# Planes of the split weight tiles 64 bytes longer: another SBUF alignment for each buffer

## The chip, the cores and the metric

The kernel runs on one core of a Trainium2 chip. The metric is device time in microseconds of one execution. Five engines work in parallel and wait for one another by semaphores: PE (TensorE, the matmuls), DVE (VectorE), ACT (ScalarE), POOL (GpSimd) and SP, which here issues most of the DMAs. SBUF is the on-chip memory with 128 partitions; an address below is the byte offset of a tile within each partition. PSUM receives the matmuls' results.

## The reference

One layer of a diffusion backbone in float32: 512 latent tokens of width 1024, 256 context tokens, 8 query and 2 key/value heads of 128.

```
hx = modulate(rms_norm(x, norm1_g), sh1, sc1)        # sh, sc, g from silu(c) @ w_mod
qx, kx, vx, ux, gx = project(hx, w_in)               # 1024 -> 4608; q, k normed, rotary
attn = block_attention(qx, [kc, kx], [vc, vx])       # softmax over 768 keys
y_a = attn @ w_attn_out
y_b = silu(layer_norm(depthwise_conv(glu(ux), 31))) @ w_conv_out
x = x + g1 * ((sigmoid(g_a) * y_a + sigmoid(g_b) * y_b) @ w_out)
hx2 = modulate(rms_norm(x, norm2_g), sh2, sc2)
x = x + g2 * ((gelu(depthwise_conv(a, 3)) * b) @ w_down)   # a, b = hx2 @ w_up, 2 x 2816
return rms_norm(x, final_g)
```

## The kernel before

Every large product is made of three matmuls in the type float32r. A float32 operand is split into a high part (a cast to float32r by ACT, line 181) and a low part (source minus high part, by DVE, line 182), and `mm3` (lines 202 to 206) adds high x high, high x low and low x high into one PSUM bank. So each step over 128 input channels is three matmuls, on lines 204, 205 and 206, mostly with 512 moving columns, and before each of them its own stationary operand of 128 x 128 is loaded (PEld in the rows).

The weights arrive in chunks of 8 KB per partition in `raw` tiles (three buffers). `weights` (line 192) splits a chunk into tiles named hl: two planes of 1024 floats, the high part and the low part, in four buffers that are taken in turn. An hl tile is stationary where the output has channels on the partitions (gates, attention output, up projection: out<-s,hl in the rows, the moving operand first) and moving where the output has tokens on the partitions (queries, output projection, down projection: out<-hl,s). The other operand is nearly always one of the 19 slots s0 to s18 (two planes of 512 floats), which hold the activations. A few others play that part in places: ex, e0 and e1 (ex holds one of four channel blocks of the convolution and later one block of the output projection, and all three are among the 14 places for the activations of the feed-forward part), and in the attention stage va (values), pT (high parts of the transposed probabilities) with y or plo (their low parts; y also holds the low parts of the values).

The stages follow each other in the program's order, with the convolution's taps on DVE laid under the projections and the attention: modulation and projections, attention (about 125 to 290 us of the span), gates and branches (to about 430), output projection and norm, up and down projection in three groups of 11, 7 and 4 channel blocks. The order on each engine is fixed when the program is built.

Where a tile lies follows from the order in which the pools are opened. At the bottom of SBUF a scratch area for DMA descriptors is reserved (16,384 bytes by default), then 128 bytes of constants; then come the four hl buffers, the slots, the cb tiles, vectors and small tiles, and the rest. The starts before:

| tile | start | length | start modulo 512 |
|---|---|---|---|
| hl, four buffers | 16512, 24704, 32896, 41088 | 8192 | 128, 128, 128, 128 (both planes) |
| s0 to s18 | 49280, then every 4096 | 4096 | 128 |
| cb0 to cb3 | 127104, then every 4224 | 4224 | 128, 256, 384, 0 |
| ident, ones | 145216, 145728 | 512 | 320 |
| va | 147680, ... | 512 | 224 |
| raw, y, plo, ex, e0, e1, pT, tmp | from 158560 on | | 352 |

All offsets of a matmul's operands within these tiles are multiples of 512 bytes, so that the start of an operand modulo 512 is that of its plane.

Of the kernel before, what the change touches and what calls it, by code (L numbers as in the profile page):

```python
# [10 lines left out]
F32R = mybir.dt.float32r  # L11
# [4 lines left out]
P = 128  # L16
# [143 lines left out]
def body(tc, x_d, ctx_d, wts_d, vecs_d, rows_d, rope_d, out_d, at):  # L160
    nc = tc.nc
# [3 lines left out]
    def pool(name, bufs=1, stack=es, **kw):  # L165
        return stack.enter_context(tc.tile_pool(name=name, bufs=bufs, reuse_waits="tile", **kw))
# [4 lines left out]
    hlp = pool("hlp")  # L171
# [8 lines left out]
    def split(src, hi, lo):  # L180
        a = S.copy(hi, src)  # L181
        b = V.tensor_tensor(lo, src, hi.bitcast(F32), ALU.subtract)  # L182
        return a.ins, b.ins

    def fetch(name, n=CH):
        raw = wp.tile([P, CH], F32, tag="raw", name="raw", bufs=3)
        nc.sync.dma_start(raw[:, :n], wts_d[at[name], :, :n])
        return raw
# [3 lines left out]
    def weights(name, w, n=CH):  # L192
        raw = fetch(name, n)
        out = []
        for o in range(0, n, 1024):
            m = min(1024, n - o)
            t = hlp.tile([P, 2, 1024], F32R, tag="hl", name="hl", bufs=4)
            done[:] = split(raw[:, o : o + m], t[:, 0, :m], t[:, 1, :m])
            out.append(t[:, :, :m].rearrange("p a (k c) -> p a k c", c=w))
        return out  # L200
# [169 lines left out]
    with ExitStack() as p0:  # L370
# [101 lines left out]
        for op in FIRST.split():  # L472
            n = int(op[1])
            if op[0] == "x":
                for t in range(TT):
                    nc.sync.dma_start(xt[t], x_d[tok(t), :])
                for t in range(TT):
                    normed(xt[t], xt[t], flat(slot[8 + t]))
            elif op[0] == "m":
                mod_x(n)  # L480
            elif op[0] == "r":
                with ExitStack() as q:
                    for i in after:
                        q.enter_context(tc.issue_after(i))
                    rows_x(n)
            elif op[0] == "w":
                wu[n] = weights(("u", n), P)
                after = list(done)
            else:
                u_mm("ab".index(op[0]), (2 * n, 2 * n + 1))  # L490
# [70 lines left out]
        for k in range(4):  # L561
            split(raw[:, 512 * k : 512 * k + 512], qT[k][:, 0], qT[k][:, 1])
        wk = qT[0:4], weights(("kv", 1), 512)
        for t in range(TT):
            project(pk[t], wk[0], hx, 0, t)
# [21 lines left out]
        def conv_u(i):  # L587
            w = weights(("u", i), P)
            for g in range(2):
                o = acc()  # L590
                for k in range(KT):
                    mm3(o, w[g][:, :, k], hx[k], k == 0, k == KT - 1)
                    if k == 3:
                        yield
                if g == 0:
                    tb = glu_b(o)
                else:
                    glu_a(i, tb, o)
                yield
# [21 lines left out]
        t = 0  # L621
# [16 lines left out]
    with ExitStack() as p1:  # L638
# [49 lines left out]
        t = 0  # L688
# [372 lines left out]
```

## Time and profile before

| | us |
|---|---|
| median of 3 runs | 840.84 (840.52 to 840.9) |
| profiled execution | 838.52 |
| its span, first to last instruction | 836.7 |
| PE busy | 818.0 |
| DVE busy | 566.5 |
| ACT busy | 362.1 |
| mean granted clock of PE | 0.998 |

The span is what the trace covers. Busy time is the time in which an engine has at least one instruction under way; matmuls overlap one another, so a busy PE says little on what one matmul costs. For that one reads the starts: the distance in time from the start of a matmul to that of the next is called a step below. PEld, the loading of stationary operands, runs beside the matmuls.

### The profile page before, as it was taken

The page shows a single profiled execution, that of the slowest core. Times are in us where ns is not written, and L with a number is a line of the kernel's source. Part 1 is how long each engine was busy: PE and PEld are TensorE (multiplying, and loading weights), DVE is VectorE, ACT ScalarE, POOL GpSimd, SP SyncE. Part 2 cuts the span into 40 slices and gives each one's busy share as a digit, 9 for nine tenths or more (in the row PEclk, how much of TensorE's full clock was granted, in tenths as well). Part 3 has the DMA queues.
Part 4 walks back from the last instruction along what each step waited for, and adds up shares of the span by engine and source line. Part 5 has one row for each costly group of instructions (what it writes and reads, how often), then busy time and mean ns, then how long its engine had stood idle before and what let it go on. Part 6 is the DMA issues. An engine that isn't in the chain of part 4 may idle for free.

```text
span 836.7 us, 10190 instructions
## 1 busy us (share of the span) xinstructions
PE 818.0 (98%) x3948; PEld 669.3 (80%) x3948; DVE 566.5 (68%) x979; ACT 362.1 (43%) x700; POOL 25.2 (3%) x50
## 2 busy tenths in 40 slices
PE   6999999999999999999999999999999999999995
PEld 2588888878888888888878988888888888888884
DVE  2578878999999997963855377755244555346565
ACT  3454455789776223523515653333122333213333
POOL 1001010000000000000000000000000000000001
PEclk9999999999999999999999999999999999999999
DMA  8861112020102336573730124542222222222102
GB/s 358 307 268 49 51 56 96 4 99 1 51 1 105 126 149 250 209 280 115 259 144 0 52 101 151 201 151 88 89 101 101 100 101 89 89 100 101 51 1 101
DMA packets 16177, 99.25 MB, mean 119 GB/s; under 512 B 1792, under 2 KB 2048, under 8 KB 6144
## 3 DMA queue, kind: packets, MB, share of 16 engines
q1 hardware_dynamic: 15120, 95.98, 31.1%
q10 hardware_dynamic: 1008, 2.62, 0.9%
q8 instruction: 31, 0.51, 0.2%
q14 instruction: 18, 0.15, 0.1%
HBM read 96.49 MB, written 2.10 MB: 118 GB/s over the span
## 4 chain that ended last, share of the span: by engine, by line
PE 91%; DVE 4%; ACT 2%; DMA 1%; issue 1%; POOL 0%; POOLq 0%; SPq 0%
PE acc L204 24%; PE acc L206 24%; PE acc L205 24%; PE bank L205 3%; PE bank L206 3%; PE bank L204 3%; PE tr L715 2%; DMA raw<-in_wts 1%; PE sc L204 1%; PE sc L206 1%; PE sc L205 1%; PE acc L426 1%; DVE s L182 1%; PE acc L431 1%; PE tr L403 1%
## 5 line engine op out<-in xcount | busy, mean ns | idle before, releaser
L204 PE MATMUL acc<-s,hl 128*128 128x512 f32 (+1 forms) x632 | 242.0, 384 | 0.6 <-ACT s L181 0.6
L206 PE MATMUL acc<-s,hl 128*128 128x512 f32 (+1 forms) x632 | 239.5, 379 | 0.0
L205 PE MATMUL acc<-s,hl 128*128 128x512 f32 (+1 forms) x632 | 239.3, 379 | 0.0
L182 DVE TENSOR_TENSOR hl<-raw,hl 128x1024 fp32r<-128x1024 f32 x118 | 139.1, 1185 | 77.4 <-ACT hl L181 76.9
L181 ACT CAST hl<-raw 128x1024 fp32r<-128x1024 f32 x118 | 119.4, 1021 | 148.9 <-PE acc L206 126.9
L204 PEld LDWEIGHTS acc<-s,hl 128*128 128x128 f32 x632 | 118.7, 188 | 23.6 <-issue 1.0
L205 PEld LDWEIGHTS acc<-s,hl 128*128 128x128 f32 x632 | 119.1, 188 | 22.7 <-issue 1.2
L206 PEld LDWEIGHTS acc<-s,hl 128*128 128x128 f32 x632 | 119.0, 188 | 22.5
L532 DVE SCALAR_TENSOR_TENSOR cb<-cb,vecs 128x512 f32<-128x512 f32 x120 | 88.4, 745 | 1.1
L204 PE MATMUL acc<-hl,s 128*128 128x512 f32 (+1 forms) x212 | 82.3, 388 | 0.2 <-DVE tmp L343 0.2
L206 PE MATMUL acc<-hl,s 128*128 128x512 f32 (+1 forms) x212 | 81.9, 387 | 0.0
L205 PE MATMUL acc<-hl,s 128*128 128x512 f32 (+1 forms) x212 | 81.9, 386 | 0.0
L961 DVE TENSOR_SCALAR tmp<-ap,vecs 128x512 f32<-128x512 f32 x22 | 12.0, 547 | 60.0 <-ACT ap L958 60.0
L958 ACT COPY ap<-acc 128x512 f32<-128x512 f32 x22 | 12.9, 588 | 77.9 <-PE acc L206 77.9
L204 PEld LDWEIGHTS acc<-hl,s 128*128 128x128 f32 x212 | 39.9, 188 | 8.3 <-PE sc L206 0.4
L206 PEld LDWEIGHTS acc<-hl,s 128*128 128x128 f32 x212 | 39.9, 188 | 8.3 <-DVE s L182 0.3
L205 PEld LDWEIGHTS acc<-hl,s 128*128 128x128 f32 x212 | 39.9, 188 | 7.6
L255 DVE SCALAR_TENSOR_TENSOR part<-raw,cs,part 128x512 f32<-128x512 f32 x56 | 41.9, 749 | 1.0
L182 DVE TENSOR_TENSOR s<-tmp,s 128x128 fp32r<-128x128 f32 (+2 forms) x67 | 29.2, 465 | 14.5 <-ACT s L181 14.4
L652 ACT ACTIVATE pr<-sc,ss,qs 128x768 f32<-128x768 f32 x32 | 31.9, 997 | 5.5 <-DVE ss L651 3.6
L964 ACT ACTIVATE tmp<-tmp 128x512 f32<-128x512 f32 x22 | 13.9, 633 | 46.5 <-DVE tmp L963 46.4
L965 DVE TENSOR_TENSOR tmp<-tmp,acc 128x512 f32<-128x512 f32 x22 | 15.1, 686 | 27.9 <-PE acc L206 27.9
(251 smaller groups left out, 1191.0 us busy)
## 6 DMA issues: line engine op xcount, KB each, us to landing
raw<-in_wts SPq DMA_DIRECT2D x78, 1024.0 KB, 4.9
raw<-in_wts SPq DMA_DIRECT2D x8, 768.0 KB, 4.2
cb<-in_x SPq DMA_DIRECT2D x8, 512.0 KB, 7.1
y<-in_ctx SPq DMA_DIRECT2D x2, 512.0 KB, 7.5
raw<-in_wts SPq DMA_DIRECT2D x2, 512.0 KB, 3.9
y<-in_rows ACTq DMA_DIRECT2D x2, 512.0 KB, 4.7
out<-o ACTq DMA_DIRECT2D x4, 256.0 KB, 2.8
out<-o SPq DMA_DIRECT2D x4, 256.0 KB, 2.6
```

The lines of the kernel that those rows point to most:

```text
L181: a = S.copy(hi, src)
L182: b = V.tensor_tensor(lo, src, hi.bitcast(F32), ALU.subtract)
L204: PE.matmul(out, lhsT=l[0], rhs=r[0], start=start, stop=False)
L205: PE.matmul(out, lhsT=l[0], rhs=r[1], start=False, stop=False)
L206: PE.matmul(out, lhsT=l[1], rhs=r[0], start=False, stop=stop)
L255: yield V.scalar_tensor_tensor(part, r[:, k], s, part, ALU.mult, ALU.add)
L532: yield V.scalar_tensor_tensor(cacc[i], cin[i][:, j : j + T], w, cacc[i], ALU.mult, ALU.add)
L652: S.activation(pt, sc, AF.Exp, bias=mx, scale=r, accum_out=sm)
L715: PE.transpose(pt[:, tok(t)], pr[h, t][:, tok(s)], ident)
L958: S.copy(ap1[:, 1 : T + 1], a)
L964: S.activation(cv, cv, AF.Gelu_apprx_tanh)
L965: V.tensor_tensor(cv, cv, b, ALU.mult)
```

## The change

The hl tile gets planes of 1040 floats in place of 1024; still only the first 1024 of each are written and read. A plane is 4160 bytes long, a tile 8320. To make room for the 512 bytes more, the scratch area is cut to 1,024 bytes.

```
-            t = hlp.tile([P, 2, 1024], F32R, tag="hl", name="hl", bufs=4)
+            t = hlp.tile([P, 2, 1040], F32R, tag="hl", name="hl", bufs=4)
...
-    nc = bacc.Bacc("TRN2", target_bir_lowering=False, num_devices=1)
+    nc = bacc.Bacc("TRN2", target_bir_lowering=False, num_devices=1, dynamic_dma_scratch_size=1024)
```

The instructions of every engine and their order stay the same. All tiles after the hl buffers move down by 14,848 bytes, which is 29 x 512, so they keep their starts modulo 512. The hl buffers now start at 1152, 9472, 17792 and 26112: their high planes at 128, 256, 384 and 0 modulo 512, their low planes at 192, 320, 448 and 64.

For two matmuls that follow each other on PE, the distance d is the start of the second one's stationary operand, minus the start of the first one's moving operand, modulo 512 bytes. Counted over all pairs of float32r matmuls in the built program (the first matmul with 512 moving columns / with 256):

| d | before | after |
|---|---|---|
| 0 | 2840 / 289 | 792 / 113 |
| 32, 64, 96, 128 | 8 / 8 | 686 / 68 |
| 160, 192 | 5 / 0 | 206 / 16 |
| 224 | 107 / 14 | 34 / 14 |
| 256 | 15 / 0 | 406 / 32 |
| 288 | 116 / 0 | 83 / 0 |
| 320 | 0 / 0 | 209 / 16 |
| 352, 384, 416 | 17 / 0 | 432 / 32 |
| 448, 480 | 0 / 0 | 260 / 20 |

## Rows read from the trace of the kernel before

**Rows 1.** The page: busy time of each engine; busy tenths in 40 slices; granted clock

```profile
PE 818.0 (98%) x3948; PEld 669.3 (80%) x3948; DVE 566.5 (68%) x979; ACT 362.1 (43%) x700; POOL 25.2 (3%) x50
...
DVE  2578878999999997963855377755244555346565
ACT  3454455789776223523515653333122333213333
...
PEclk9999999999999999999999999999999999999999
```

**Rows 2.** The chain that ended last, by engine

```profile
PE 91%; DVE 4%; ACT 2%; DMA 1%; issue 1%; POOL 0%; POOLq 0%; SPq 0%
```

**Rows 3.** Groups by form, splits into hl: busy us, mean ns; idle before, releasers

```profile
L181 ACT CAST hl<-raw 128x1024 fp32r<-128x1024 f32 x110 | 114.6, 1050 | 144.7 <-PE acc L206 122.8 <-DMA raw<-in_wts 13.8 <-issue 7.9
...
L182 DVE TENSOR_TENSOR hl<-raw,hl 128x1024 fp32r<-128x1024 f32 x110 | 133.9, 1221 | 77.4 <-ACT hl L181 76.9
```

**Rows 4.** Timeline of PE, up projection, first and last of sixteen: start us, length us

```profile
504.66 0.39 PE L206 MATMUL acc<-s,hl 128*128 128x512 f32 x1
...
508.06 0.39 PE L206 MATMUL acc<-s,hl 128*128 128x512 f32 x1
```

**Rows 5.** Timeline, a matmul and the load beside it

```profile
505.11 0.39 PE L205 MATMUL acc<-s,hl 128*128 128x512 f32 x1
505.12 0.19 PEld L206 LDWEIGHTS acc<-s,hl 128*128 128x128 f32 x1
```

**Rows 6.** Timeline of PE, down projection, second group: first and tenth of ten

```profile
728.95 0.40 PE L206 MATMUL acc<-hl,s 128*128 128x512 f32 x1
...
731.05 0.39 PE L206 MATMUL acc<-hl,e 128*128 128x512 f32 x1
```

**Rows 7.** Tile hl on PE, 725 to 752 us: length ns min/median/max

```profile
L204 PE MATMUL acc<-hl,s x19: 389/390/390, 725.7 to 750.6; 128*128 128x512 f32 x19
...
L204 PE MATMUL acc<-hl,e x14: 393/396/397, 725.0 to 752.0; 128*128 128x512 f32 x14
```

**Rows 8.** Tiles ex and plo on PE, as moving operands: length ns min/median/max

```profile
L205 PE MATMUL acc<-ex,hl x8: 397/397/398, 380.1 to 415.7; 128*128 128x512 f32 x8
...
L205 PE MATMUL acc<-plo,s x24: 392/397/404, 217.8 to 274.0; 128*128 128x512 f32 x24
```

**Rows 9.** Tiles va and s on PE, attention stage: length ns min/median/max

```profile
L205 PE MATMUL acc<-y,va x24: 387/394/479, 153.3 to 215.0; 128*128 128x512 f32 x24
...
L205 PE MATMUL acc<-hl,s x11: 388/397/399, 151.0 to 167.0; 128*128 128x512 f32 x11
```

**Rows 10.** Timeline of PE, attention stage, two steps in which va is loaded

```profile
188.30 0.39 PE L204 MATMUL acc<-pT,va 128*128 128x512 f32 x1
188.52 0.39 PE L205 MATMUL acc<-y,va 128*128 128x512 f32 x1
...
205.01 0.39 PE L204 MATMUL acc<-s,hl 128*128 128x512 f32 x1
205.24 0.39 PE L205 MATMUL acc<-y,va 128*128 128x512 f32 x1
```

**Rows 11.** Timeline of PE, two steps in which ones is loaded

```profile
287.80 0.39 PE L206 MATMUL acc<-s,hl 128*128 128x512 f32 x1
288.03 0.59 PE L294 MATMUL acc<-part,ones 128*128 128x512 f32 x1
...
310.46 0.39 PE L206 MATMUL acc<-s,hl 128*128 128x512 f32 x1
310.69 0.59 PE L793 MATMUL acc<-ln,ones 128*128 128x512 f32 x1
```

**Rows 12.** Line 979, residual adds: length ns min/median/max

```profile
L979 DVE TENSOR_TENSOR cb<-cb,tmp x25: 418/691/695, 612.5 to 830.3; 128x512 f32<-128x512 f32 x23, 128x256 f32<-128x256 f32 x2
```

**Rows 13.** The page: DMA issues by line and engine, KB each, us to landing

```profile
raw<-in_wts SPq DMA_DIRECT2D x78, 1024.0 KB, 4.9
...
out<-o ACTq DMA_DIRECT2D x4, 256.0 KB, 2.8
```

## The prediction

> **What bounds the kernel now.** I read the page first. [...] The chain that ended last is PE for 91%, DVE 4%, ACT 2%, DMA 1% [rows 2]: what lengthens or shortens a matmul arrives almost whole at the end. DVE stands idle 77.4 us before its splits into hl, nearly all of it until ACT is done, and ACT 144.7 us before its own, mostly until PE is [rows 3]: the engines that write the changed tile have slack. So the question is what one matmul costs, and for that its shown length misleads: a 512-column matmul is listed with 0.39 us, but matmuls overlap, and each costs the time from one start to the next. In a plain stretch sixteen of them start between 504.66 and 508.06: fifteen steps in 3.40 us, 226.7 ns each [rows 4]. That is the unit of the sum.
>
> **What the change touches.** Every engine issues the same instructions in the same order; no wait and no DMA is added, and every tile but hl keeps its start modulo 512. Only hl's planes start elsewhere. While a matmul streams its moving operand, the stationary operand of the next one is loaded: the load starts at 505.12 and lasts 0.19 us, beside the matmul that started at 505.11 [rows 5]. PE thus reads two places of SBUF at once, and their distance d (defined with the table in the section on the change) is what the change alters. Before, d is 0 for 2,840 of 3,108 steps of 512 columns; after, for 792.
>
> The trace of before holds a natural experiment on d. The tiles ex, e0 and e1 start at 352 modulo 512, hl and the slots at 128. Where ex or e is stationary and hl moves, d is 224. Nine such steps run from 728.95, the last matmul on a slot, under which ex is loaded, to 731.05: 2.10 / 9 = 233.3 ns each, 6.6 more than in the plain stretch [rows 6]. The lengths agree: 396 ns median with e against 390 with a slot, on the same line in the same 27 us, and the slot's hardly scatter (389 to 390) [rows 7]. Where ex moves over a stationary hl, d is 288: 397 ns; plo moving over a slot, also d = 288: 397 [rows 8]. So a step at d of 224 or 288 costs 6.6 ns more.
>
> It is not 352 by itself. In the attention stage y starts at 352 too, and where it moves and the next load is y (d = 0) the length goes down to 387 ns; plo over a slot never goes below 392 [rows 8, 9]. At 188.30 a step with d = 384 (pT moving, va loaded) takes 0.22 us; at 205.01, with d = 96 (a slot moving, va loaded), 0.23; at 287.80 and 310.46, with d = 192 (a slot moving, ones, at 320, loaded), 0.23 [rows 10, 11]. So the price is seen at 224 and 288 and not at 0, 96, 192 and 384: a region about half of 512. One group disturbs the picture: from 151 to 167 us matmuls of hl over slots, at d = 0, have a median of 397 [rows 9]. DVE is busy for nine tenths of that slice and ACT for seven or more [rows 1], and their company may cause the same extra by itself, before as after.
>
> [...]
>
> **The sum**, in steps that a region of d gains or loses (512 and 256 columns together, at one price, since the load is the same):
> - A, d = 256: 15 before, 438 after, 423 more. No row shows an ordinary matmul there; 224 and 288 on either side cost 6.6. Ends 0 and 6.6 ns; I take 6.6: 423 x 6.6 ns = +2.79 us.
> - B, d = 224 or 288: 237 before, 131 after (where ex, e or plo now meets another distance): 106 x 6.6 ns = -0.70 us.
> - C, d = 320: none before, 225 after. 288, 32 bytes away, costs 6.6; 384, 64 away, costs nothing, nor does 192, its mirror about 256. Ends 0 and +1.49 us; its neighbours disagree, so I take half, +0.75.
> - D, the other new distances (32 to 192, 352 to 480): about 1,680 more steps. The shortest length in rows 9 is 387, 3 ns under 390; the longer steps of rows 10 and 11 read 0.23, at face value 3.3 over the plain one. Ends -5.0 and +5.5 us; I take 0, since the four steps average 227.5, the plain one within their rounding.
>
> Together +2.84 us on PE. About 7% of the chain is DVE, ACT and DMA [rows 2]; there PE waits, and a longer matmul may vanish in it. Times 0.95: +2.7 us.
>
> The rest I cost at nothing. A split that writes hl might change with its address; but the residual adds run over cb0 to cb3, which start at 128, 256, 384 and 0, at a median of 691 ns and at most 695 [rows 12]. Even 2% on all 110 splits of 1221 ns would be 2.7 us, under the 77.4 us of slack [rows 3]; without that cover, where DVE sets the pace in the attention stage, it is some 24 ns for each of a few tiles. The smaller scratch at the bottom of SBUF is used by no instruction of the kernel: its transfers are all issued by SP and ACT [rows 13] and stay as they are.
>
> The profiled execution took 838.52 us (its span of 836.7 and 1.8 around it), so 841.2 with the sum. The median of the runs is 2.3 above it: 840.84 + 2.7 = 843.5.
>
> **Rivals.**
> - *Alignment as such, or nothing.* The price belongs to starts that are no multiple of 64 bytes (352 = 5.5 x 64), whatever the other operand is. The new starts are all multiples of 64, and ex, e and plo stay at 352: A to D are 0, and the time is 840.8. For it: rows 6 to 8 involve 352 every time. Against it: y over y at 387 [rows 9]. [...]
> - *Graded.* The price grows with the distance from 0: 6.6 at 224, so 7.5 at 256, 5.7 at 192 and 320, 3.8 at 128 and 384, 1.9 at 64 and 448. Summed over the table this is +9.4 us, times 0.95: 849.8. Against it: the steps at 192 and 384 show nothing of the kind [rows 10, 11].
> - *Relief (not slower).* At d = 0 both reads start in the same place, and a part of the 226.7 ns comes from that. Every distance away from 0 and from the half then saves, at most D's 3 ns: -5.0 + 2.84 = -2.2, times 0.95, 838.8; if 256 is harmless as well, 836.1. It decides from 1.7 ns a step (2.84 us / 1,680). For it: 387 in rows 9. Against it: slots and hl at d = 0 reach 387 too, and the four steps are not below the plain one.
> - That the layout stays as it is: excluded, the four buffers follow each other and each is 128 bytes longer.
>
> **How the numbers follow.** Forecast 0.47, alignment as such or nothing 0.28, graded 0.12, relief 0.13. A difference of 0.2%, about what a measurement of this kernel can tell from no change, is 1.7 us. The forecast's own range is 841.5 to 847: A less B without C and with D at a quarter of its lower end, up to A and C full with D at half its upper end; nine tenths of it is slower. With the graded case that is 0.54 slower; the null case and the forecast's lower edge give 0.31 same; relief and scatter 0.15 faster. The range goes from 839.5, which leaves out the stronger half of relief, to 848.0, which leaves out the graded case.
>
> **What the profile of after would show.** Under the forecast, matmuls on three of the four hl buffers keep 390 ns, and on the buffer 256 away from the slots two of each three show 396 or more; in the up projection, stretches of 227 ns steps and of steps up to 234 follow each other as the buffers change. A part of e's and ex's matmuls falls to 390. PE's share stays at 98%, DVE's and ACT's busy time stays. Wrong would be: one median on all four buffers; a price on the buffer 128 or 384 away too; a buffer clearly under 389; or time in a wait that is not there now.

## The result and the profile after

The kernel after takes 850.25 us (849.26 to 853.07, four runs) against 840.87 for the kernel before beside it: a ratio of 1.0126, 95% interval 1.0108 to 1.0145. It is 9.4 us slower; the forecast was +2.7 us, and the time lies above the range, beside the graded rival's 849.8.

The profiled execution took 850.48 us, with a span of 848.7 against 836.7, 12.0 us more. The page after, in the same rows as [rows 1, 2] (busy us, share and count of each engine; granted clock by slices; the chain that ended last):

```profile
PE 829.2 (98%) x3948; PEld 669.9 (79%) x3948; DVE 566.8 (67%) x979; ACT 362.2 (43%) x700; POOL 25.2 (3%) x50
...
PEclk9999999999999999999999999999999999999998
...
PE 92%; DVE 3%; ACT 2%; DMA 2%; issue 1%; POOL 0%; POOLq 0%; SPq 0%
```

Only PE has grown, by 11.2 us; DVE and ACT are within 0.3 us of before. The splits into hl, which write the changed tile, take what they took in [rows 3] (groups by form: busy us, mean ns; idle before, and releasers):

```profile
L182 DVE TENSOR_TENSOR hl<-raw,hl 128x1024 fp32r<-128x1024 f32 x110 | 134.0, 1221 | 78.7 <-ACT hl L181 78.5
L181 ACT CAST hl<-raw 128x1024 fp32r<-128x1024 f32 x110 | 114.7, 1050 | 148.2 <-PE acc L206 128.0 <-DMA raw<-in_wts 10.7 <-issue 8.2
```

So the time is in the steps of PE. In the up projection each hl buffer serves 24 matmuls in a row. Five rows of PE's timeline after (start us, length us): the first matmul on the buffer with high plane at 128 modulo 512, then on those at 0, at 384, at 256, and at 128 again:

```profile
504.57 0.39 PE L204 MATMUL acc<-s,hl 128*128 128x512 f32 x1
...
510.11 0.39 PE L204 MATMUL acc<-s,hl 128*128 128x512 f32 x1
...
515.69 0.39 PE L204 MATMUL acc<-s,hl 128*128 128x512 f32 x1
...
521.22 0.39 PE L204 MATMUL acc<-s,hl 128*128 128x512 f32 x1
...
526.80 0.39 PE L204 MATMUL acc<-s,hl 128*128 128x512 f32 x1
```

At 226.7 ns a step [rows 4] 24 steps would take 5.44 us. Here they take 5.54, 5.58, 5.53 and 5.58. Two things are to be seen. The third buffer, 256 from the slots, is no dearer than the first, whose high plane is in step with them. And the first pays too, although its high plane has not moved: its low plane has.

In the down projection, the tile hl in the same work as [rows 7] (lengths ns, min/median/max, first and last start):

```profile
L204 PE MATMUL acc<-hl,s x19: 390/393/397, 736.4 to 761.4; 128*128 128x512 f32 x19
...
L204 PE MATMUL acc<-hl,e x14: 389/395/397, 735.0 to 760.7; 128*128 128x512 f32 x14
```

With a slot loaded the median went from 390 to 393 and the lengths scatter; with e loaded it went from 396 to 395.

Matching the pairs of neighbouring matmuls of the two traces (3,817 pairs) and adding the differences of their steps gives 11.5 us. 10.7 of them lie in 2,922 steps of 512 columns that wait for nothing, -0.4 in the 256-column steps, -0.3 in steps with a wait. 1.5 us lie in float32 matmuls at 20 to 23 us, where the granted clock fell from 1.00 to a mean of 0.58 (0.50 from 20.5 us on), after 2 us in which PE was busy for 1.02 (windows of after: length; busy us and instructions of PE, PEld, DVE, ACT, POOL; granted clock; DMA share; GB/s):

```profile
18.00:20.00 2.00, 1.02 (x12) 0.68 (x15) 0.89 (x3) 0.25 (x1) 0.55 (x2) 1.00 0.78 291
20.00:23.00 3.00, 3.00 (x25) 1.90 (x18) 1.69 (x3) 2.52 (x5) 0.00 (x0) 0.58 0.62 218
```

In twelve of the thirteen runs below these float32 steps take what they took before, within 0.01 us; the thirteenth, a kernel that pays nothing (all tiles moved together), has the same 1.5 us. So they belong to the one execution. What made the clock fall is not shown: the run with the scratch alone has the same 1.02 us of PE in the 2 us before, and its clock stays at 1.00. The start of the program differs too: the first matmul began at 7.38 in place of 6.15 us, both times on the arrival of the first weights, and the first 32 matmuls then took 8.47 us in place of 8.94 (over all 3,947 pairs of neighbours the differences come to 11.0 us). Without these three the 12.0 us of the profile come to 9.7, beside the 9.4 of the medians.

### The profile page after: what moved, and what is told of

Same layout as the page of the kernel before. It is cut to its first block, busy times and chain, and to the rows that moved or that the text cites. A ratio compares the mean times of both kernels' runs of the same rounds, so it can differ in the third digit from the quotient of the medians.

```text
span 848.7 us, 10190 instructions
## 1 busy us (share of the span) xinstructions
PE 829.2 (98%) x3948; PEld 669.9 (79%) x3948; DVE 566.8 (67%) x979; ACT 362.2 (43%) x700; POOL 25.2 (3%) x50
## 4 chain that ended last, share of the span: by engine, by line
PE 92%; DVE 3%; ACT 2%; DMA 2%; issue 1%; POOL 0%; POOLq 0%; SPq 0%
PE acc L206 25%; PE acc L204 24%; PE acc L205 24%; PE bank L205 3%; PE bank L206 3%; PE bank L204 3%; PE tr L715 2%; DMA raw<-in_wts 2%; PE sc L204 1%; PE sc L206 1%; PE sc L205 1%; PE acc L426 1%; PE tr L403 1%; PE acc L431 1%; PE acc L266 0%
```

## The experiments

All kernels differ from the kernel before by the edit shown alone; each median stands beside one of before from the same chip (where none is given, the last one given). Where an edit needs room, the scratch is cut to 1,024 bytes, as in the change, or set so that the tiles keep their starts. For each, the rows are the first matmul on the first hl buffer of the same five as above and the one 96 steps on, so that the difference divided by 96 is one step with hl stationary, in the first of the three groups of the up projection. Before, it is 226.7 ns [rows 4]. "Distance" is d taken modulo 256: loaded operand minus moving operand.

**The scratch alone.**

```
+    nc = bacc.Bacc("TRN2", ..., num_devices=1, dynamic_dma_scratch_size=1024)
```

> The smaller scratch alone, hl planes of 1024 floats as before: every tile moves down by 15,360 bytes and keeps its start modulo 512. Region (the forecast's theory: a step pays 6.6 ns only where d is near half of 512), graded (price grows with d) and quantum (a step pays one fixed amount of about 6.7 ns as soon as its stationary operand or the next one loaded starts elsewhere modulo 256 than its moving operand) all expect the time of before, 840.9. A rival in which the scratch or the absolute addresses matter expects most of the +9.4 here: about 850.

839.98 against 839.95, ratio 1.0006 (0.9996 to 1.0015).

```profile
500.18 0.39 PE L204 MATMUL acc<-s,hl 128*128 128x512 f32 x1
...
521.93 0.39 PE L204 MATMUL acc<-s,hl 128*128 128x512 f32 x1
```

21.75 / 96 = 226.6 ns. The second line of the diff, and with it a shift of all tiles by 30 x 512 bytes, does nothing.

**Everything behind hl 128 bytes later, the planes as before.**

```
+    gap = cst.tile([P, 32], F32, name="gap")
     slot = [cst.tile([P, 2, T], F32R, name=f"s{i}") for i in range(19)]
...
+    nc = bacc.Bacc("TRN2", ..., num_devices=1, dynamic_dma_scratch_size=15360)
```

> hl as before, but everything behind it, the slots included, moved up by 128 bytes, so that all four hl buffers, both planes, are 128 away from the slots (some 2,850 steps with hl). Region: nothing, 840.5 (the ex and e steps leave their d of 224 too). Graded: 3.8 ns a step, +10, 851. Quantum: 6.7 ns on every step with hl, 2,850 x 6.7 x 0.95 = +18, 859.

851.25, ratio 1.0137 (1.0122 to 1.0152), +11.3 us.

```profile
504.19 0.39 PE L204 MATMUL acc<-s,hl 128*128 128x512 f32 x1
...
526.50 0.39 PE L204 MATMUL acc<-s,hl 128*128 128x512 f32 x1
```

22.31 / 96 = 232.4 ns, 5.7 more. The forecast's region, with no price at 128, is out. The rest of the trace says the same: of all steps of 512 columns at this distance, 513 have neither DVE nor ACT at work beside them and average 232.5 ns, and 1,946 have, and average 232.5. So this price is not that of the company of other engines, which I had suspected in [rows 9]; those rows themselves come up again in the run with every operand in step.

**The same by 256 bytes** (the gap is 64 floats long).

> The same with 256 bytes: all hl steps at d = 256. Region: 6.6 ns on each, +18, 859. Graded: 7.5 ns, +20, 861. Quantum with a period of 256 bytes: nothing, 840.9, steps of 226.7 ns throughout.

839.8, ratio 0.9994 (0.9985 to 1.0004).

```profile
498.93 0.39 PE L204 MATMUL acc<-s,hl 128*128 128x512 f32 x1
...
520.69 0.39 PE L204 MATMUL acc<-s,hl 128*128 128x512 f32 x1
```

21.76 / 96 = 226.7 ns, with d = 256 modulo 512 in nearly every step. This ends the forecast's term A as I reasoned it, and the graded rival, which had its peak here, though it had the time of the run with 128 bytes right (851): 256 bytes apart cost nothing here.

**The high plane in step, the low plane 64 bytes further, in all four buffers.**

```
-            t = hlp.tile([P, 2, 1024], F32R, tag="hl", name="hl", bufs=4)
+            t = hlp.tile([P, 2176], F32R, tag="hl", name="hl", bufs=4)[:, 0:2080].rearrange("p (a x) -> p a x", a=2)
```

> hl tiles of 8704 bytes with the low plane 4160 bytes behind the high one: in all four buffers the high plane keeps d = 0, the low plane is 64 away; no rotation from buffer to buffer. Region: 841. Graded: 1.9 ns on the third of the steps that load a low plane (or move it), +1.8, 842.6. Quantum: of the three steps of a product the one under which the low plane is loaded and the one in which it is stationary pay, 2/3 x 2,850 x 6.7 x 0.95 = +12, 853.

848.97, ratio 1.0109 (1.0094 to 1.0124). The rows as for the others, then the three lines of the product in the same group (lengths ns, min/median/max):

```profile
503.70 0.39 PE L204 MATMUL acc<-s,hl 128*128 128x512 f32 x1
...
525.89 0.39 PE L204 MATMUL acc<-s,hl 128*128 128x512 f32 x1
```

```profile
L205 PE MATMUL acc<-s,hl x128: 392/392/393, 499.8 to 589.5; 128*128 128x512 f32 x128
L206 PE MATMUL acc<-s,hl x128: 392/397/398, 500.0 to 589.8; 128*128 128x512 f32 x128
L204 PE MATMUL acc<-s,hl x128: 389/389/793, 500.2 to 590.0; 128*128 128x512 f32 x128
```

Over the 96 steps, 22.19 / 96 = 231.1 ns, or 693.4 a product of three in place of 680: 13.4 more, of which the starts of all such steps after 300 us put 8 to 9 on line 206, about 3 on line 205 and 1 on line 204; the lengths say the same (397, 392 and 389). Only one load of the three (the low plane's, beside the matmul of line 205) is out of step, and most of the price stands one step later, on line 206, whose own distance is 0. None of the three times expected (841, 842.6, 853) was right.

**Everything behind hl 64 bytes later** (gap of 16 floats).

> All tiles behind the hl buffers move up by 64 bytes, the planes keep their length: every distance between hl and a slot is 64 or 448. If any difference modulo 256 costs a step the same (quantum), the price lies between that of 128 bytes away (5.7 ns a step, +11.3 us) and that of 32 bytes away (6.6 to 6.8 ns): +11 to +13.5 us, 851 to 854. If the price grows with the distance from a multiple of 256 and is largest at 128 (graded modulo 256), 64 costs half of it, 2.9 ns: +5.7 us, 846. If what was paid in the kernel after came from the high and the low plane standing apart, and not from hl against the slots: 840.

846.18 against 840.02, ratio 1.0071 (1.0053 to 1.0089).

```profile
502.69 0.39 PE L204 MATMUL acc<-s,hl 128*128 128x512 f32 x1
...
524.66 0.39 PE L204 MATMUL acc<-s,hl 128*128 128x512 f32 x1
```

21.97 / 96 = 228.9 ns. That looks like the graded answer, but it is half of the truth: the steps after 300 us in which hl moves and a slot is loaded (distance 64) average 233.4 ns, those in which hl is stationary (distance 192, or 64 the other way) 229.0. In this run the sign counts, or else whether hl moves or is loaded.

**Both planes of hl 16 bytes later.**

```
+            t = hlp.tile([P, 2176], F32R, tag="hl", name="hl", bufs=4)[:, 4:2052].rearrange("p (a x) -> p a x", a=2)
```

> Both planes of hl start 16 bytes later, inside a longer tile: every distance between hl and a slot is 16 or 496, the smallest so far. If any difference modulo 256 costs the same: 5 to 7 ns a step, +10 to +14 us, 850 to 854. If operands within the same 32 or 64 bytes count as being in step (threshold): no price, 840.

848.49, ratio 1.0097 (1.0079 to 1.0115).

```profile
505.36 0.39 PE L204 MATMUL acc<-s,hl 128*128 128x512 f32 x1
...
527.75 0.39 PE L204 MATMUL acc<-s,hl 128*128 128x512 f32 x1
```

22.39 / 96 = 233.2 ns. 16 bytes cost as much here as any distance so far, so that the threshold of the expectation is not seen in this group.

But the price does not last. In the second and third groups of the up projection the same slots move, from the same addresses, over hl tiles in the same places; two rows from the second group, 96 steps apart:

```profile
663.28 0.39 PE L204 MATMUL acc<-s,hl 128*128 128x512 f32 x1
...
685.04 0.39 PE L204 MATMUL acc<-s,hl 128*128 128x512 f32 x1
```

21.76 / 96 = 226.7 ns, the step of before. In all, 427 such steps of the first group average 233.3 ns, and 526 of the other two 226.7. So the starts of the operands do not set the price alone; this is also why the whole run, below the 850 to 854 expected, came to less than others with steps of 233. What else decides is not shown.

**The change with 256 bytes in place of 64** (the slice is 0:2176, so that the low plane starts 4,352 bytes behind the high one).

> The change with 256 bytes in place of 64: the low plane of hl starts 256 bytes further (modulo 512) than the high plane, which stays at 128 in all four buffers. If only the difference modulo 256 counts: no price, steps of 227 ns on all three lines, 840. If it is the planes standing apart that costs (as they did by 64 in the run before and paid 13.4 ns a product): +9 us, 849.

839.81, ratio 0.9997 (0.9986 to 1.0008).

```profile
499.76 0.39 PE L204 MATMUL acc<-s,hl 128*128 128x512 f32 x1
...
521.52 0.39 PE L204 MATMUL acc<-s,hl 128*128 128x512 f32 x1
```

21.76 / 96 = 226.7 ns: planes may stand apart, by 256 bytes. The tile is longer here than in the change, and the scratch as small: neither costs anything by itself.

**Every operand of PE at 128 modulo 256.**

```
+    gap1 = cst.tile([P, 16], F32, name="gap1")
     ident = cst.tile([P, P], F32, name="ident")
...
+    gap2 = cst.tile([P, 24], F32, name="gap2")
     vs = [...]
...
+    gap3 = cst.tile([P, 32], F32, name="gap3")
     yp = pool("yp")
```

> Three gaps of 64 to 128 bytes put every operand that PE reads (hl, slots, ident, ones, va, and y, plo, pT, ex, e) at 128 modulo 256; nothing else changes but the smaller scratch. If a difference modulo 256 is what costs, the 237 steps of before at 224 and 288 and some 20 others lose 6.6 ns each: 257 x 6.6 = 1.7 us on PE, nine tenths of it at the end, 0.9980 to 0.9985 of before (838.4 to 838.9 beside 840). ex, e and plo then show 390 ns in place of 396. If those steps are slow for another reason (their tiles' own place or their writers): no change, 840.

838.88 against 840.02, ratio 0.9993 (0.9978 to 1.0008): the medians are 1.1 us apart in the expected direction, but the interval holds 1, so a gain is not shown by the times. The steps show it. The lines of [rows 7] and the first of [rows 8] in this run (lengths ns, min/median/max):

```profile
L204 PE MATMUL acc<-hl,s x19: 389/389/389, 725.7 to 750.1; 128*128 128x512 f32 x19
...
L204 PE MATMUL acc<-hl,e x14: 389/389/389, 725.0 to 751.5; 128*128 128x512 f32 x14
```

```profile
L205 PE MATMUL acc<-ex,hl x8: 389/389/390, 380.4 to 415.8; 128*128 128x512 f32 x8
```

396 and 397 have become 389. Summed over the matched steps PE saves 0.9 us, a little over half of the 1.7 expected. In the up projection, where nothing was out of step, nothing moves:

```profile
498.77 0.39 PE L204 MATMUL acc<-s,hl 128*128 128x512 f32 x1
...
520.53 0.39 PE L204 MATMUL acc<-s,hl 128*128 128x512 f32 x1
```

21.76 / 96 = 226.7 ns.

The slow group of [rows 9], hl over slots in the attention stage, stays slow in the main with every operand in step. The median on line 205 falls from 397 to 389, but on the other two lines it stays above:

```profile
L206 PE MATMUL acc<-hl,s x11: 387/393/397, 151.9 to 167.6; 128*128 128x512 f32 x11
L204 PE MATMUL acc<-hl,s x10: 389/397/476, 152.2 to 167.1; 128*128 128x512 f32 x10
```

Over the whole attention stage, steps of 512 columns at distance 0 (those over 260 ns left out) average 229.7 ns in this run and 229.5 before, against 226.7 and 226.8 from the up projection on. So something other than the distance also makes steps longer there; what it is, the company of other engines or the order of unlike matmuls, is not shown.

**Everything behind hl 192 bytes later** (gap of 48 floats).

> The mirror of the run with 64: all tiles behind the hl buffers move up by 192 bytes, so the stationary hl now starts 64 beyond the moving slot (modulo 256) and the stationary slot 64 short of the moving hl. Sign theory (what counts is the start of the loaded operand minus that of the moving one, modulo 256, with its sign; +64 cost 6.4 ns a step and -64 cost 2.0): 1,445 steps of stationary hl at 6.4 and 478 of moving hl at 2.0 after 300 us of the span, in all 10 us, 850; steps of stationary hl 233 ns, of moving hl 229. Role theory (a moving hl pays more than a stationary one whatever the sign): the same as with 64, 846.

851.47 against 839.65, ratio 1.0145 (1.0130 to 1.0160).

```profile
503.76 0.39 PE L204 MATMUL acc<-s,hl 128*128 128x512 f32 x1
...
526.16 0.39 PE L204 MATMUL acc<-s,hl 128*128 128x512 f32 x1
```

22.40 / 96 = 233.3 ns with a stationary hl at distance 64, as the moving hl had in the run with 64 bytes: the sign theory holds there, and the role theory falls. At 192 the moving hl's steps now average 231.8, though, where 229.0 was expected, and the whole came to 11.8 us in place of 10. That average mixes two prices. Two rows of the first group of the down projection and two of the second, 24 steps apart each:

```profile
606.27 0.40 PE L204 MATMUL acc<-hl,s 128*128 128x512 f32 x1
...
611.87 0.40 PE L204 MATMUL acc<-hl,s 128*128 128x512 f32 x1
...
746.22 0.39 PE L204 MATMUL acc<-hl,s 128*128 128x512 f32 x1
...
751.72 0.39 PE L204 MATMUL acc<-hl,s 128*128 128x512 f32 x1
```

5.60 / 24 = 233.3 ns, and 5.50 / 24 = 229.2. All 263 such steps of the first group average 233.3, those of the other two groups 229.0 and 229.4. Again one distance has two prices in one run, and the sign theory fits only one of them.

**The low plane 192 bytes further** (the slice is 0:2144).

> The low plane of hl 192 bytes (modulo 256) from the high plane, the high plane in step with the slots. Where hl is stationary one load of three is 64 short of the moving operand. Jump theory (operands that jump from one distance to another pay about 6.7 ns for each way, as in the run with 64, 13.4 ns a product): again +9 us, 849. Sign theory alone (each load pays by its own distance: 2.0 ns where hl is stationary, 6.4 where it moves): 2.0 ns a product on 479 products and 6.4 on some 160, +2 to +3 us, 842.5.

847.26, ratio 1.0092 (1.0077 to 1.0107), +7.6 us.

```profile
501.94 0.39 PE L204 MATMUL acc<-s,hl 128*128 128x512 f32 x1
...
524.13 0.39 PE L204 MATMUL acc<-s,hl 128*128 128x512 f32 x1
```

22.19 / 96 = 231.1 ns, 13.4 a product once more, where each load paying for its own distance would give 2. The distance between a matmul's own two operands, which is also 64 short in one matmul of three, would give the same 2 and is out with it. The jump theory holds where hl is stationary; over the whole kernel its +9 is nearer than +2 to +3, but not met.

**Both planes 4 bytes later** (the slice is 1:2049).

> Both planes of hl start a single element, 4 bytes, later. If any difference modulo 256 puts the two reads out of step: 2 to 6 ns a step, +5 to +11 us, 845 to 851. If a unit of 16 bytes or less is what counts: 840. In the latter case the price of the run with 16 bytes begins between 4 and 16.

854.57, ratio 1.0182 (1.0166 to 1.0197): +14.9 us, the dearest of all and above the range expected, for one element.

```profile
506.44 0.39 PE L204 MATMUL acc<-s,hl 128*128 128x512 f32 x1
...
528.75 0.39 PE L204 MATMUL acc<-s,hl 128*128 128x512 f32 x1
```

22.31 / 96 = 232.4 ns where hl is stationary; where it moves (distance 252) the steps average 237.0.

**All tiles 128 bytes on, together.**

```
+    nc = bacc.Bacc("TRN2", ..., num_devices=1, dynamic_dma_scratch_size=15488)
```

> A scratch of 15,488 bytes moves every tile by the same 128 bytes modulo 512: hl and the slots start at a multiple of 256 in place of 128 beyond one, all distances stay as before. If only the distance between the two reads counts: 840, steps of 227 ns. If the place of each operand itself counts (a multiple of 256 or 512 better than 128): a gain, with ex, e and plo, now at 480, still at 396 ns.

840.12, ratio 1.0006 (0.9989 to 1.0024).

```profile
500.83 0.39 PE L204 MATMUL acc<-s,hl 128*128 128x512 f32 x1
...
522.59 0.39 PE L204 MATMUL acc<-s,hl 128*128 128x512 f32 x1
```

21.76 / 96 = 226.7 ns. The common place itself, a multiple of 256 or half of one, made no difference.

**The low planes of hl and of the slots both 64 bytes further** (the edit of the run with the low plane 64 bytes further, and the slots cut in the same way from tiles of 1088 floats; the lines of the product are 205 to 207 here).

```
+    slot_t = [cst.tile([P, 1088], F32R, name=f"s{i}") for i in range(19)]
+    slot = [t[:, 0:1056].rearrange("p (a x) -> p a x", a=2)[:, :, 0:T] for t in slot_t]
```

> The low planes of hl and of the slots both 64 bytes from their high planes. Under each moving high plane a high plane is loaded and under each moving low plane a low plane: every load is in step (distance 0 modulo 256) with the operand that moves beside it, in 2,804 steps; but in two matmuls of three the stationary operand's start and that of its own moving operand differ by 64. If the distance between a load and the operand that moves beside it is all that counts: no price, 840. If operands whose places jump from matmul to matmul pay as such, as the 13.4 ns a product of the run with the low plane of hl alone may suggest: that run's +9 us or more, 849 to 855.

847.9 against 839.47, ratio 1.0097 (1.0079 to 1.0115).

```profile
503.25 0.40 PE L205 MATMUL acc<-s,hl 128*128 128x512 f32 x1
...
525.43 0.40 PE L205 MATMUL acc<-s,hl 128*128 128x512 f32 x1
```

22.18 / 96 = 231.0 ns, 13.3 a product, although every load is at distance 0 from the operand that moves beside it. So the price is also paid where no load starts apart from the operand that moves beside it: here the starts change from one matmul to the next, and the price is that of the run with the low plane of hl alone, 13.4. The whole came to 8.4 us, a little under the +9 or more expected.

Side by side, for the first group of the up projection (the steps with a stationary hl take the same in the other two groups, but for the run with 16 bytes):

| starts modulo 256 | ns a step | ns a product | us against before |
|---|---|---|---|
| all equal (before; scratch alone; 256 twice; all 128 on) | 226.7 | 680 | -0.2 to +0.5 |
| slots 64 beyond hl | 228.9 | 687 | +6.2 |
| low plane of hl 64, or 192, beyond the rest | 231.1 | 693 | +9.0, +7.6 |
| low planes of both 64 beyond | 231.0 | 693 | +8.4 |
| slots 128 beyond hl | 232.4 | 697 | +11.3 |
| hl 4 beyond the slots | 232.4 | 697 | +14.9 |
| hl 16 beyond the slots | 233.2 (other groups 226.7) | 700 (680) | +8.5 |
| slots 192 beyond hl | 233.3 | 700 | +11.8 |

## Why the prediction was wrong

The first part stood. PE bounds the kernel (98% busy, 92% of the chain); DVE, ACT and the splits did not move; a cost on a matmul arrives nearly whole (10.25 us in the steps by the table below, 9.4 in the time). The price of a step out of step, 6.6 ns from [rows 6], was of the right size: the runs give 0 to 10 for a step with its operands apart, and mostly 5 to 7. The sum failed on where it is paid. By the terms of the prediction, with what the matched steps of before and after differ by:

| term | forecast us | measured us | steps of 512 columns, mean change |
|---|---|---|---|
| A, d = 256 | +2.79 | +1.66 | 390 at +4.3 ns |
| B, 224 and 288 left | -0.70 | -0.13 | 99 at -1.3 |
| C, d = 320 | +0.75 | +0.60 | 209 at +2.9 |
| D, the other distances | 0 | +6.67 | 1,430 at +4.7 |
| d unchanged | none | +1.89 | 794 at +2.4 |
| 256 columns | in A to D | -0.44 | 295 (of 256 columns), D's 128 at -3.2 |

They add up to 10.25 us; times the prediction's 0.95 that is 9.7, against 9.4 measured. So the step that failed is D, taken at 0 "since the four steps average 227.5, the plain one within their rounding". Three things were wrong with that reading. The rows give starts to 0.01 us, which is more than the 6.6 ns in question, so that one step can't show it; it takes the sum over many. The step that I read is that of the load out of step, while most of the price stands in the next one (8 to 9 ns on line 206, about 3 on line 205, in the run with the low plane 64 bytes further); after all four steps of [rows 10, 11] comes a matmul of another kind (on va, or in float32 on ones with 0.59 us), so that those rows hold no plain next step to compare. And D's upper end, 3.3 ns x 1,680, was itself taken from the rounded rows, so that the range had no room for what [rows 6] already showed at 6.6.

The second failure is the term that wasn't there. A pair whose d stayed 0 was counted as untouched, but the run with the low plane of hl 64 bytes further, where line 206 pays most at a distance of 0, and the run with both low planes moved show that d of a single pair is not the whole matter: after the change the high planes in step with the slots are read between low planes that are not. By these two runs, this is the 1.89 us, and why the first buffer above takes 5.54 us.

The sign of A was right by accident. 256 bytes cost nothing (run with 256 bytes, 839.8 against 839.95 and 226.7 ns a step); the 390 steps counted there have low planes 64 bytes off as neighbours, as in the run with the low plane 64 bytes further, and pay as there. B gave back a fifth, since ex, e and plo were out of step before and mostly still are. The steps of 256 columns do not pay at all, where I charged them like the long ones; D's 128 became 3.2 ns shorter.

Of the rivals, graded came nearest in time (849.8) and is wrong in mechanism: its dearest distance, 256, cost nothing (226.7 ns a step), and 4 bytes cost more than 64 (+14.9 us and +6.2). That it met the time is chance. Alignment as such and relief fall with the run at 128 bytes, 232.4 ns a step against 226.7 with nothing changed but where the operands start, and the one with all tiles moved, 226.7.

What stays open is the machinery. In the up projection the price of a product comes as 6.7, 13.4 or 20 ns (one, two or three times 6.67) in six of the eight runs that pay, and as 17.2 in the other two; which of them a set of starts gives, and why 64 one way can cost three times as much as 64 the other way, none of the runs tells. Nor do the starts settle it: in the run with 16 bytes the same operands at the same addresses pay 6.6 ns a step in the first group of the up projection and nothing in the other two, and in the run with 192 bytes the moving hl pays 6.6 in the first group of the down projection and 2 to 3 after it. What came before on PE may decide; no run tests that.

## What to carry to other kernels

Give all operands that PE reads in a run of matmuls the same start modulo 256 bytes, planes of one tile included: in each run here with equal starts in the up projection a step there took 226.6 to 226.7 ns, whether the common start is 0 or 128 made no difference (840.12 us against 839.65), a pad of 256 bytes cost nothing (839.81 against 840.02), and one of 4 to 192 bytes cost 1 to 3% of a step in the first group of the up projection (nothing later in the run with 16) and 0.7 to 1.8% of the kernel. In a kernel that is 98% PE, read the cost of a matmul from start to start over dozens of steps: a few ns a step are below the rounding of any single row, 0.01 us.

## What was not expected of the hardware

- Operands 256 bytes apart pay nothing (226.7 ns a step), and the finest grain tried, 4 bytes, is the dearest (237.0 ns a step at distance 252, 232.4 at 4).
- The price can depend on the sign: at 64 a step takes 233.3 to 233.4 ns in both runs that have it throughout, at 192 it takes 229.0 in one, and 233.3 or 229.0 to 229.4, by the group, in the other.
- One set of starts can have two prices in one run: at distance 16, 427 steps average 233.3 ns and 526 later ones 226.7.
- Steps of 256 columns (119.3 ns before) don't pay; in the run with 128 bytes 289 of them take 0.7 ns less than before, in that with 192 bytes 287 take 3.5 ns less.
- DVE and ACT at work beside a step did not change its price at 128 bytes (232.5 ns with and without). At distance 0 in the attention stage steps average 229.5 to 229.7 ns for a reason that is not shown.
